# The modulation vectors of a two-block transformer: products on three engines in place of 32-column matmuls

## The chip, the cores and the metric

The kernel is one program on one core of one Trainium2 chip. The metric is the device time of one execution in microseconds (us), from the first to the last instruction and what the runtime lays around them. A core has TensorE (PE; its weight loads, which overlap the matmuls, are listed as PEld), VectorE (DVE), ScalarE (ACT), GpSimd (POOL) and SyncE (SP, which here issues most loads). Each engine runs its own instructions in order and waits for the others through semaphores. SBUF is the on-chip memory, PSUM the eight banks that TensorE writes.

## What is computed

Two blocks run one after the other on 512 latent tokens and 256 context tokens of width 1024, in float32. Each block is steered by modulation vectors: a conditioning vector goes through silu and is multiplied by a 1024 x 6144 matrix, and the product is cut into six vectors of 1024.

```python
s_lat = jax.nn.silu(c)
s_ctx = jax.nn.silu(c_ctx)
m_lat = jnp.split((s_lat @ w_mod[l] + b_mod[l])[:, None, :], 6, axis=-1)
m_ctx = jnp.split(s_ctx @ w_mod[l] + b_mod[l], 6, axis=-1)
h_lat = modulate(rmsnorm(x_lat, norm1_g[l]), m_lat[0], m_lat[1])
...
x_lat = x_lat + m_lat[2] * (mix_lat @ w_out[l])
h_lat = modulate(rmsnorm(x_lat, norm2_g[l]), m_lat[3], m_lat[4])
x_lat = x_lat + m_lat[5] * expert_choice_ffn(h_lat, ...)
```

The first block mixes tokens in four ways (neighbourhood attention, a gated delta net, differential attention, a Fourier transform) and goes through 16 experts. The second block has a state-space branch, an attention branch and a gated feed-forward net, and is modulated in the same way by `w_mod_2`.

## The kernel before

The kernel is a generator program. Pieces of work are Python generators; `weave` and `beside` interleave them in program order, and a list scheduler then orders each engine's instructions: of those whose inputs are there by its own model of time, the one that stands first in the program goes next. Matmul helpers record every operation under one line (L367), copies out of PSUM under L393 (ScalarE) and L395 (VectorE), loads under L398, so operations are told apart by their tiles.

The first two modulation vectors of the first block are made at the very start (`a_in`, bank tag `md`). All the others are made in `g_mods`: vectors 2, 3, 4, 5 of the first block and 0, 1, 3, 4, 2, 5 of the second. It runs beside `g_ft` (Fourier) and `g_na` (neighbourhood attention), and all three are woven with `g_dn`, the gated delta net. Behind them come `g_df` (differential attention) and `g_wo`, still beside `g_dn`; then the output projection, the choice of tokens, the experts with the context's part of the second block beside them, and the second block.

A vector is two blocks of 512 columns. `mod_rows` makes one: four loads of [128, 2, 512] (512 KB each) from a ring of three buffers in the pool `mods`, and eight float32 matmuls, each with a padded stationary of 32 columns (column 0 the latent's silu, column 1 the context's, the rest zero) and a 512-column slice of the weights as the moving operand. Contraction tile kt goes to the 32 PSUM partitions 32 (kt % 4), so one bank collects four partial rows for each of the two conditioning vectors. A copy (L393 and L395 in turn) takes the bank to SBUF. From there:

- `mod_bcast` (vectors used as a gate along the free axis): a matmul with the 0/1 matrix `k_sel` adds the four partial rows and spreads the sum over all partitions; VectorE adds the bias (L516).
- `mod_cols` (channels on partitions): four transposes a block (L490), a reduction (L491), the bias (L492).
- `mod_cols_pk` (channel 8 p + kt at [p, kt]): eight matmuls a block with a strided stationary of 64 columns into the bank `bigbank`, which `g_na` also takes its scores from; then a reduction (L503).
- the gates of the second block: `k_sel` again, the bias added in one partition (L644), stored to DRAM (`gtd`).

`g_dn` goes through 12 chunks, two at a time: `ind` inverts a triangular matrix of each chunk in a row of short steps (64x64 matmuls into `bank_dn`, a copy on ScalarE at L970, transposes at L957, products on GpSimd at L948 and additions on VectorE at L978), and `rec` takes the state from chunk to chunk (`bank_dnr`, one copy a chunk at L1001).

Of the kernel before, what the change touches and what calls it, by code (L numbers as in the profile page):

```python
# [9 lines left out]
F = np.float32  # L10

# ---------------------------------------------------------------- host layout
# [11 lines left out]
def _pack_cols(inp):  # L24
    parts, off = ([], []), [0, 0]
# [5 lines left out]
    g = lambda n: np.asarray(inp[n])  # L31
# [24 lines left out]
def _na_bias(rpb):  # L56
    rpb = np.asarray(rpb)[0]                          # [4, 15, 31]
# [14 lines left out]
    return np.ascontiguousarray(np.stack(out, 1).astype(F))      # [128, 12, 256]  # L72


def _consts():
# [3 lines left out]
    ang = np.concatenate([(t // 64)[:, None] * inv, (t % 64)[:, None] * inv], 1)    # [512, 16]  # L79
    cs = np.stack([np.cos(ang), np.sin(ang)], 1)                                    # [512, 2, 16]  # L80
# [23 lines left out]
    ang = np.stack([(t // 64)[:, None] * inv, (t % 64)[:, None] * inv], 1)          # [512, 2, 16]  # L104
    cs = np.stack([np.cos(ang), np.sin(ang)], 1)                                    # [512, 2, 2, 16]
    K["k_rope2"] = np.ascontiguousarray(cs.reshape(4, 128, 64).transpose(1, 0, 2)).astype(F)
    K["k_m"] = np.ascontiguousarray(np.concatenate(cols, 1)).astype(F)
    sel = np.zeros((128, 128))
    sel[[0, 32, 64, 96]] = 1.0
    K["k_sel"] = sel.astype(F)  # L110
# [21 lines left out]
class Arena:  # L132
    """SBUF of one core as a free list over one tile: alloc and free in program order."""
# [34 lines left out]
class Duo:  # L168
    """Two arenas as one."""
# [10 lines left out]
class Pool:  # L180
    """SBUF whose pieces are tiles of their own, all released together."""
# [12 lines left out]
class Buf:  # L194
    """A piece of an arena or a tile of a pool, seen as [128, *shape]."""
# [31 lines left out]
class Part(Buf):  # L227
    """A piece of a buffer."""
# [9 lines left out]
class Ring:  # L238
    """n equal buffers taken in turn."""
# [15 lines left out]
class Bag:  # L255
    """Equal buffers, given out and taken back; the one that came back first goes out first."""
# [12 lines left out]
    # buffers for a while, until shed  # L269
# [14 lines left out]
class Split:  # L284
    """A block of weights as two exact parts: part i of tile kt along the contraction."""
# [13 lines left out]
def weave(*gens):  # L299
    """Runs generators side by side; each yields the work it has put out, as a part of all of its own."""  # L300
# [9 lines left out]
def ranked(tc, gen, off):  # L310
    """gen's pieces, issued as if they stood off instructions further on."""
# [16 lines left out]
def beside(main, total, fill):  # L328
    """main's pieces, which yield total, and fill's, which yield 1, at the same pace."""
# [13 lines left out]
def filled(tc, main, fill):  # L343
    """main's pieces; each yields how much of fill goes in behind it, and maybe the instruction it stays behind."""
# [14 lines left out]
class KA:  # L359
# [5 lines left out]
    # ---------------------------------------------------------------- helpers  # L365
# [48 lines left out]
    # ---------------------------------------------------------------- set up  # L414
    def setup(self, cx):
# [14 lines left out]
        self.m2c_b = Buf(M, [4, 8, 2])                  # sh1, sc1, sh2, sc2 of the second block  # L430
        self.ab2_b = Buf(M, [3, 8])                     # norm gains: block 1 lat, ctx; block 2
# [12 lines left out]
    # a stage's SBUF as a free list  # L444
# [10 lines left out]
    # r ** -0.5 * f of a few columns  # L455
# [5 lines left out]
    # silu(c) columns of two vectors as a padded stationary [128, 8, 32]  # L461
# [2284 lines left out]
```

## Time and profile before

| what | value |
|---|---|
| timed runs, median of 3 | 3065.87 us (3064.37 to 3069.57) |
| profiled execution, first to last instruction | 3070.7 us |
| mean granted TensorE clock, share of full speed | 0.983 |
| TensorE matmuls busy | 2908.0 us, 95% |
| VectorE, ScalarE, GpSimd busy | 1341.8, 911.1, 631.7 us |
| stage with `g_mods` (223 to 455 us) | 232 us |
| stage with `g_df` (455 to 655 us) | 200 us |

The profiled execution lies 4.8 us (0.16%) above the median of the timed runs and 1.1 us above the highest of them. In the rows below, a group of instructions is given by line, engine and operation, then output <- inputs by tile names, shapes (partitions x elements), count, busy time in us, mean ns of one, and the idle time of the engine ahead of them with what ended it. A float32 matmul stands as two instructions. Busy time is a union: overlapping instructions count once. Shares are of the window that is named.

### The profile page before, as it was taken

Reading aid. Unit: us, or ns where it says so; the run is one execution under the profiler, and the core shown is the slowest. Engines: PE = TensorE matmul, PEld = TensorE weight load, DVE = VectorE, ACT = ScalarE, POOL = GpSimd, SP = SyncE. Lnnn points to the kernel's source line nnn. Section 1 sums busy time; section 2 is a strip of 40 time slices with the busy share of each in tenths; the row PEclk is TensorE's granted clock in tenths of the full one; section 3 lists DMA queues with packets and bytes.
Section 4 is the critical chain, followed back from the end, with each engine's and each line's share of the span. In section 5 each row is a group of like instructions: output and inputs, shape, how many; then the busy total and the mean of one; then the engine's idle time right before and its main releaser. Section 6 shows DMA issues by size and latency. Waiting matters only on the chain.

```text
span 3070.7 us, 42582 instructions
## 1 busy us (share of the span) xinstructions
PE 2908.0 (95%) x17172; PEld 1918.0 (62%) x17172; DVE 1341.8 (44%) x2673; ACT 911.1 (30%) x1855; POOL 631.7 (21%) x662
## 2 busy tenths in 40 slices
PE   7999999998999999899999989999999999999998
PEld 4894557756454544244343358787878778878887
DVE  5522546654221211011011057869696945364445
ACT  5511226532111010000000034445454444253333
POOL 3121225521000000000000023323232323242232
PEclk8999999999999999999999989999999999999999
DMA  7216660147979797999999943323332275242231
GB/s 261 75 46 200 206 197 23 35 155 290 371 311 386 318 368 321 423 431 430 431 430 431 430 152 102 103 84 100 86 105 82 87 251 174 94 153 96 96 102 57
DMA packets 255428, 652.01 MB, mean 212 GB/s; under 512 B 15672, under 2 KB 168760, under 8 KB 230656
## 3 DMA queue, kind: packets, MB, share of 16 engines
q1 hardware_dynamic: 212368, 600.95, 51.6%
q10 hardware_dynamic: 42864, 48.35, 4.7%
q8 instruction: 135, 2.21, 0.3%
q14 instruction: 61, 0.50, 0.1%
HBM read 627.61 MB, written 21.64 MB: 211 GB/s over the span
## 4 chain that ended last, share of the span: by engine, by line
PE 61%; DVE 8%; DMA 5%; ACT 2%; issue 1%; POOL 1%; POOLq 0%; DVEq 0%; ACTq 0%
PE bank_mm L367 25%; PE bigbank L367 22%; PE bank_pj L367 6%; PE bank_c L367 3%; DMA b<-in_w_down 2%; DMA l<-in_w_up 1%; PE bank_sm L367 1%; PE bank_y L367 1%; DMA wo<-in_w_down 1%; PE bank_mm L2146 1%; DVE mix L2395 1%; DVE base L2391 1%; DVE mix L2394 1%; DVE c L1929 1%; DMA l<-in_w_down 1%
## 5 line engine op out<-in xcount | busy, mean ns | idle before, releaser
L367 PE MATMUL bank_pj<-c,c 128*128 128x512 f32 (+2 forms) x1368 | 317.7, 375 | 0.0
L367 PE MATMUL bank_mm<-c,c 128*128 128x512 f32 (+1 forms) x1608 | 304.4, 347 | 2.5 <-DVE c L1929 1.3
L367 PEld LDWEIGHTS bank_mm<-c,c 128*128 128x128 f32 x1608 | 259.3, 191 | 42.1 <-DVE c L1929 1.7
L367 PEld LDWEIGHTS bank_pj<-c,c 128*128 128x128 f32 (+1 forms) x1368 | 225.1, 188 | 48.3 <-issue 15.4
L367 PE MATMUL bank_mm<-l 128*128 128x128 f32 (+3 forms) x944 | 229.1, 499 | 4.2 <-DVE l L395 2.0
L1928 ACT CAST c<-base 128x1024 fp32r<-128x1024 f32 x147 | 152.8, 1045 | 254.7 <-PE bigbank L367 105.7
L1929 POOL TENSOR_TENSOR c<-base,c 128x1024 fp32r<-128x1024 f32 x47 | 115.7, 2462 | 453.3 <-ACT c L1928 393.5
L367 PEld LDWEIGHTS bank_mm<-l 128*128 128x128 f32 (+2 forms) x944 | 155.6, 246 | 75.3 <-issue 66.6
L367 PE MATMUL bigbank<-l 128*64 128x512 f32 (+1 forms) x864 | 198.1, 586 | 4.5 <-DMA l<-in_w_up 2.8
L1929 DVE TENSOR_TENSOR c<-base,c 128x1024 fp32r<-128x1024 f32 x100 | 134.9, 1351 | 137.6 <-ACT c L1928 132.8
L367 PEld LDWEIGHTS bigbank<-l 128*64 128x64 f32 (+1 forms) x864 | 62.8, 141 | 117.9 <-issue 105.2
L1676 DVE TENSOR_TENSOR b<-l,bigbank 128x512 f32<-128x512 f32 x32 | 20.6, 684 | 255.7 <-PE bigbank L367 225.7
L367 PE MATMUL bank_c<-b 128*128 128x256 f32 (+3 forms) x496 | 119.2, 385 | 12.6 <-ACT b L1843 8.3
L1604 POOL TENSOR_TENSOR l<-l,ab 128x512 f32<-128x512 f32 x8 | 8.4, 1047 | 560.2 <-DVE l L1591 506.7
L367 PEld LDWEIGHTS bank_c<-b 128*128 128x128 f32 (+1 forms) x496 | 80.6, 194 | 54.8 <-issue 30.1
L367 PE MATMUL bigbank<-out,c 128*128 128x512 f32 x480 | 112.5, 394 | 2.4 <-ACT out L2489 1.8
L367 PE MATMUL bank_mm<-h,sp 128*128 128x512 f32 (+3 forms) x544 | 108.3, 388 | 4.2 <-ACT h L606 3.8
L367 PEld LDWEIGHTS bank_dn<-dn 64*64 64x64 f32 x1920 | 74.0, 134 | 56.4 <-issue 39.1
L367 PE MATMUL bigbank<-b,l 128*64 128x512 f32 x480 | 105.7, 593 | 2.3 <-DMA b<-in_w_up 1.2
L367 PEld LDWEIGHTS bigbank<-out,c 128*128 128x128 f32 x480 | 90.9, 190 | 22.9 <-ACT out L2489 2.0
L1600 ACT ACTIVATE l<-bank_mm,ab,ab 128x128 f32<-128x128 f32 x32 | 14.7, 458 | 292.6 <-DVE l L1602 292.4
L367 PEld LDWEIGHTS bank_mm<-h,sp 128*128 128x128 f32 (+1 forms) x544 | 85.9, 186 | 24.7 <-ACT h L606 4.0
(556 smaller groups left out, 5175.0 us busy)
## 6 DMA issues: line engine op xcount, KB each, us to landing
l<-in_w_up SPq DMA_DIRECT2D x25, 2048.0 KB, 10.6
l<-in_w_gate SPq DMA_DIRECT2D x25, 2048.0 KB, 9.6
l<-in_w_down SPq DMA_DIRECT2D x25, 2048.0 KB, 16.2
base<-in_w_in SPq DMA_DIRECT2D x90, 512.0 KB, 3.8
mods<-in_w_mod SPq DMA_DIRECT2D x80, 512.0 KB, 4.6
base<-in_w_up SPq DMA_DIRECT2D x18, 2048.0 KB, 8.6
wo<-in_w_gate SPq DMA_DIRECT2D x18, 2048.0 KB, 10.1
b<-in_w_gate SPq DMA_DIRECT2D x15, 2048.0 KB, 19.5
```

Of the source, the lines that this page charges most:

```text
L367: self.mm_ins = self.nc.tensor.matmul(out, l, r, start=start, stop=stop).ins
L1600: nc.scalar.activation(XG[:, kt], b[:, kk], AF.Identity, bias=b2[:, kt:kt + 1], scale=a2[:, kt:kt + 1])
L1604: nc.gpsimd.tensor_mul(sc, S, aff[:, :, ee, None].to_broadcast([128, 4, 2, 64]))
L1676: nc.vector.tensor_mul(hid[:, 512 * j:512 * j + 512], s, ac[1][:, j])
L1928: nc.scalar.copy(hi, raw)
L1929: (nc.vector if self.wn % 4 in self.losplit else nc.gpsimd).tensor_sub(lo, raw, hi.bitcast(F32))
L2146: nc.tensor.transpose(tb[:, z], p[:, 128 * (g0 + z):128 * (g0 + z) + 128], self.ident)
L2391: nc.vector.scalar_tensor_tensor(E[:, h], rw[:, h, 0], gc(1, 0, h), E[:, h], op0=OP.subtract, op1=OP.min)
L2394: nc.vector.tensor_scalar(W[:, h], cb[:, c, 0], gc(0, 0, h), None, op0=OP.mult)
L2395: nc.vector.scalar_tensor_tensor(W[:, h], cb[:, c, 1], gc(0, 1, h), W[:, h], op0=OP.mult, op1=OP.add)
```

## The change

`mod_rows` stays for the first two vectors. For all others a new function `mod_sums` takes its place. It multiplies each contraction tile [128, 512] of the weights by the conditioning column of that tile, one value a partition, and adds the eight products elementwise, so that one tile [128, 512] of sums over the contraction tiles is left, whose partitions have still to be added. Even tiles go to VectorE (one product, then three multiply-adds into `d`), odd tiles to ScalarE (four scaled copies), whose results GpSimd adds into `o`; a last GpSimd addition joins the two. The sum over partitions is a matmul with ones. A block is made for one conditioning vector at a time, so blocks that are wanted for the latent and the context (vectors 0 and 1 of the second block) load their weights twice.

```diff
+    def mod_sums(self, s, wdram, j, r):
+        nc, (wr, da, pa, pp) = self.nc, self.mr
+        wv = wdram.rearrange("(kt p) n -> p kt n", p=128)[:, :, j * 512:(j + 1) * 512]
+        d, o = da(), pa()
+        for k in range(0, 8, wr.per):
+            w = wr()
+            self.ld(w, wv[:, k:k + wr.per])
+            for i in range(wr.per):
+                kt = k + i
+                c = s[:, kt, r:r + 1]
+                if kt == 0:
+                    nc.vector.tensor_scalar(d, w[:, i], c, None, op0=OP.mult)
+                elif kt % 2 == 0:
+                    nc.vector.scalar_tensor_tensor(d, w[:, i], c, d, op0=OP.mult, op1=OP.add)
+                else:
+                    z = o if kt == 1 else pp()
+                    nc.scalar.activation(z, w[:, i], AF.Copy, scale=c)
+                    if kt > 1:
+                        nc.gpsimd.tensor_add(o, o, z)
+        nc.gpsimd.tensor_add(o, o, d)
+        return o
+    def mod_cols2(self, s, wdram, bname, j, rs, out):
+        nc, n = self.nc, len(rs)
+        t = self.bank((128, 8, n), self.md)
+        for h in range(2):
+            for r in rs:
+                o = self.mod_sums(s, wdram, 2 * j + h, r)
+                for c in range(4):
+                    self.mm(t[:, 4 * h + c, r:r + 1], o[:, c * 128:(c + 1) * 128], self.km("one", 1))
+        nc.vector.tensor_add(out[:, :, 0:n], t, ...)
     def mod_cols_pk(...)
-        t = self.big().rearrange("p (k g r) -> p k g r", k=8, g=4)
+        t = self.bank((128, 8), self.md)
         for h in range(2):
-            r = rows()
-            self.mod_rows(s, wdram, 2 * j + h, ring, r)
+            o = self.mod_sums(s, wdram, 2 * j + h, 0)
             for kt in range(8):
-                self.mm(t[64 * h:64 * h + 64, kt].rearrange("p g r -> p (g r)"), r[:, kt::8], self.ident)
+                self.mm(t[64 * h:64 * h + 64, kt:kt + 1], o[:, kt::8], self.km("one", 1))
     def mod_bcast(...)
-            r = rows()
-            self.mod_rows(s, wdram, 2 * j + h, ring, r)
+            r = self.mod_sums(s, wdram, 2 * j + h, 0)
             t = self.bank((128, 512), self.md)
-            self.mm(t, ksel, r)
+            self.mm(t, self.km("one"), r)
             o = out[:, h * 512:(h + 1) * 512]
             nc.vector.tensor_add(o, t, o)
+            yield 0.05
     def g_mods(self, tag, n):
-            wr, rows = Ring(P, [2, 512], n), Ring(P, [512], 2)
+            sums = [Ring(self.M, [512], k) for k in (1, 2)]
+            pp = Ring(P, [512], 2)
+            self.mr = [Ring(P, [2, 512], n)] + sums + [pp]
...
-                self.mod_cols(s2, wm, "b_mod_2", j, wr, rows, mc[:, i])
+                self.mod_cols2(s2, wm, "b_mod_2", j, (0, 1) if j < 2 else (0,), mc[:, i])
...
-                    self.mod_rows(s2, wm, 2 * j + h, wr, r)
+                    r, g = self.mod_sums(s2, wm, 2 * j + h, 0), pp()[0:1]
-                    self.mm(t, self.sel, r)
+                    self.mm(t, self.km("one"), r)
```

The rings are one buffer for `d`, two for `o`, two for ScalarE's products and, as before, three for the weights. `k_sel` and its load at the start are gone. `mod_bcast` yields after each block of 512 columns instead of after the vector. The rest of the diff takes comments out.

## Rows read from the trace of the kernel before

**Rows 1.** The page: span and number of instructions.

```profile
span 3070.7 us, 42582 instructions
```

**Rows 2.** Stages in one row each: length; busy us (instructions) by engine; clock, DMA share, GB/s.

```profile
223.00:455.00 232.00, 222.46 (x2160) 120.53 (x2156) 94.14 (x224) 56.75 (x175) 51.40 (x88) 0.99 0.63 206
455.00:655.00 200.00, 189.32 (x2396) 144.48 (x2393) 126.03 (x312) 110.42 (x305) 92.24 (x150) 0.98 0.12 42
...
655.00:1228.00 573.00, 539.07 (x2439) 275.90 (x2441) 133.21 (x280) 82.11 (x177) 54.22 (x54) 0.98 0.85 332
1228.00:1766.00 538.00, 499.57 (x2194) 210.41 (x2190) 62.99 (x107) 24.41 (x47) 3.14 (x3) 0.99 1.01 429
```

**Rows 3.** Groups of TensorE in the stage 223 to 455 us, by form.

```profile
L367 PE MATMUL bank_mm<-mods,ab 128*32 128x512 f32 x320 | 72.4, 610 | 4.7 <-DMA mods<-in_w_mod 4.7
L367 PE MATMUL bank_dn<-dn 64*64 64x64 f32 x880 | 45.4, 226 | 2.2 <-DVE base L1156 0.6 <-DVE dn L978 0.6 <-ACT dn L970 0.5
...
L367 PE MATMUL bank_mm<-mods,ab 128*128 128x512 f32 x16 | 9.9, 703 | 1.1 <-ACT mods L393 0.7 <-DVE mods L395 0.3
L367 PE MATMUL bigbank<-base,mods 128*64 128x128 f32 x64 | 8.8, 290 | 0.0
...
L367 PE MATMUL bank_mm<-l 128*128 128x512 f32 x16 | 7.2, 604 | 0.0
...
L490 PE MATMUL bank_mm<-base,mods 128*128 128x128 f32 x32 | 5.1, 283 | 0.0
```

**Rows 4.** The same view of the stage 455 to 650 us.

```profile
L367 PE MATMUL bank_mm<-l,dn 128*128 128x64 f32 x180 | 23.8, 276 | 0.0
```

**Rows 5.** Waits in 223 to 455 us: waiter <- releaser, total us, times, longest.

```profile
POOL dn L948 <- PE bank_dn L367: 80.2, 17, 10.4
...
ACT dn L970 <- PE bank_dn L367: 46.8, 21, 7.6
...
SPq L398 <- PE bank_mm L367: 125.5, 58, 6.7
```

**Rows 6.** The tile `mods`: ns min/median/max, first and last start us; then landing times.

```profile
L398 SPq DMA_DIRECT2D mods<-in_w_mod x80: 367/368/1624, 223.8 to 445.6; - x80
...
L395 DVE COPY mods<-bank_mm x10: 690/692/693, 263.8 to 451.7; 128x512 f32<-128x512 f32 x10
...
L644 DVE TENSOR_TENSOR mods<-mods,bank_mm x4: 675/676/676, 425.4 to 454.0; 1x512 f32<-1x512 f32 x4
...
DMA to landing us min/median/max: 3.7/4.6/9.0
```

**Rows 7.** Line 1001, one a chunk of `g_dn`: in 300:480, then in 460:680 us.

```profile
L1001 DVE COPY dn<-bank_dnr x5: 416/424/426, 314.5 to 469.2; 128x256 f32<-128x256 f32 x5
...
L1001 DVE COPY dn<-bank_dnr x8: 407/416/424, 469.2 to 677.6; 128x256 f32<-128x256 f32 x8
```

**Rows 8.** Groups of the whole run by form: operations like the added ones.

```profile
L1160 DVE TENSOR_SCALAR l<-l,base 128x512 f32<-128x512 f32 x16 | 8.6, 578 | 0.2
...
L2364 DVE SCALAR_TENSOR_TENSOR mix<-base,mix 128x512 f32<-128x512 f32 x32 | 22.1, 692 | 0.0
...
L1765 DVE SCALAR_TENSOR_TENSOR mix<-mix,mix 128x512 f32<-128x512 f32 x24 | 19.0, 792 | 7.0 <-ACT mix L1764 6.2
...
L2415 ACT ACTIVATE mix<-mix 128x512 f32<-128x512 f32 x8 | 5.0, 624 | 1.8 <-DVE mix L2413 1.7
...
L948 POOL TENSOR_TENSOR dn<-dn,a 128x256 f32<-128x256 f32 x60 | 45.4, 768 | 115.2 <-PE bank_dn L367 102.4 <-DVE dn L922 12.8
...
L1848 POOL TENSOR_TENSOR b<-b 128x512 f32<-128x512 f32 x16 | 16.5, 1042 | 176.1 <-ACT b L1843 119.9 <-PE bank_c L367 56.2
...
L1351 POOL TENSOR_TENSOR l<-l 128x512 f32<-128x512 f32 x8 | 11.6, 1445 | 32.0 <-DVE l L1350 32.0
```

**Rows 9.** Stretches near the start, same columns as rows 2.

```profile
10.00:20.00 10.00, 4.83 (x18) 1.24 (x16) 0.47 (x3) 2.60 (x5) 0.55 (x1) 0.69 1.03 415
...
40.00:50.00 10.00, 7.56 (x21) 5.41 (x21) 9.07 (x13) 8.51 (x14) 5.83 (x4) 0.66 0.80 277
```

More of the change, by code (lines that the diff above doesn't have):

```diff
@@ L107, in _consts @@
     K["k_m"] = np.ascontiguousarray(np.concatenate(cols, 1)).astype(F)
-    sel = np.zeros((128, 128))
-    sel[[0, 32, 64, 96]] = 1.0
-    K["k_sel"] = sel.astype(F)
     return K
@@ L492, in mod_cols @@
         nc.vector.tensor_add(out, out, self.col(bname, 8 * j, 8)[:, :, None].to_broadcast([128, 8, 2]))
-    def mod_cols_pk(self, s, wdram, bi, j, ring, rows, out):
+    def mod_sums(self, s, wdram, j, r):
[19 more added lines that the diff above has]
+        return o
@@ new lines, in mod_cols2 @@
+    def mod_cols2(self, s, wdram, bname, j, rs, out):
[6 more added lines that the diff above has]
+                    self.mm(t[:, 4 * h + c, r:r + 1], o[:, c * 128:(c + 1) * 128], self.km("one", 1))
+        nc.vector.tensor_add(out[:, :, 0:n], t, self.col(bname, 8 * j, 8)[:, :, None].to_broadcast([128, 8, n]))
@@ L496, in mod_cols_pk @@
+    def mod_cols_pk(self, s, wdram, bi, j, out):
         nc = self.nc
-        t = self.big().rearrange("p (k g r) -> p k g r", k=8, g=4)
+        t = self.bank((128, 8), self.md)
         for h in range(2):
-            r = rows()
-            self.mod_rows(s, wdram, 2 * j + h, ring, r)
+            o = self.mod_sums(s, wdram, 2 * j + h, 0)
             for kt in range(8):
-                self.mm(t[64 * h:64 * h + 64, kt].rearrange("p g r -> p (g r)"), r[:, kt::8], self.ident)
-        nc.vector.tensor_reduce(out, t[:, :, :, 0:2].rearrange("p c g r -> p c r g"), AX.X, OP.add)
@@ L504, in mod_cols_pk, with mod_bcast @@
-        nc.vector.tensor_add(out, out, self.col("b_mod_pk", 8 * bi, 8)[:, :, None].to_broadcast([128, 8, 2]))
-    def mod_bcast(self, s, wdram, bdram, j, ring, rows, out, ksel):
+                self.mm(t[64 * h:64 * h + 64, kt:kt + 1], o[:, kt::8], self.km("one", 1))
+        nc.vector.tensor_add(out[:, :, 0], t, self.col("b_mod_pk", 8 * bi, 8))
+    def mod_bcast(self, s, wdram, bdram, j, out):
         nc = self.nc
@@ L572, in a_in @@
         self.gt1_b, self.gt2_b = Buf(AB, [1024]), Buf(AB, [1024])
-        self.sel = Buf(AB, [128]).ap()
         self.md = "md"
@@ L582, in a_in @@
         self.ld(cx, I["ctx"][0].rearrange("(t p) d -> p t d", p=128), nc.scalar)
-        self.ld(self.sel, I["k_sel"], nc.scalar)
         s1, wm = self.s1b.ap(), I["w_mod"][0]
@@ L617, in g_mods @@
         with self.pool("mods") as P:
-            wr, rows = Ring(P, [2, 512], n), Ring(P, [512], 2)
+            sums = [Ring(self.M, [512], k) for k in (1, 2)]
+            pp = Ring(P, [512], 2)
+            self.mr = [Ring(P, [2, 512], n)] + sums + [pp]
             s1, wm = self.s1b.ap(), I["w_mod"][0]
             mp, a2 = self.mpk_b.ap(), self.a2_b.ap()
-            self.mod_bcast(s1, wm, I["b_mod"], 2, wr, rows, self.gt1_b.ap(), self.sel)
+            yield from self.mod_bcast(s1, wm, I["b_mod"], 2, self.gt1_b.ap())
+            self.mod_cols_pk(s1, wm, 0, 3, mp[:, 0])
             yield 0.1
-            self.mod_cols_pk(s1, wm, 0, 3, wr, rows, mp[:, 0])
-            yield 0.1
-            self.mod_cols_pk(s1, wm, 1, 4, wr, rows, mp[:, 1])
+            self.mod_cols_pk(s1, wm, 1, 4, mp[:, 1])
             nc.vector.scalar_tensor_tensor(a2, mp[:, 1, :, 0], 1.0, self.col("norm2_g_pk", 0, 8), op0=OP.add, op1=OP.mult)
             yield 0.1
-            self.mod_bcast(s1, wm, I["b_mod"], 5, wr, rows, self.gt2_b.ap(), self.sel)
-            yield 0.1
+            yield from self.mod_bcast(s1, wm, I["b_mod"], 5, self.gt2_b.ap())
             mc, a = self.m2c_b.ap(), self.ab2_b.ap()
@@ L638, in g_mods @@
                 for h in range(2):
-                    r, g = rows(), rows()[0:1]
-                    self.mod_rows(s2, wm, 2 * j + h, wr, r)
+                    r, g = self.mod_sums(s2, wm, 2 * j + h, 0), pp()[0:1]
                     t = self.bank((128, 512), self.md)
-                    self.mm(t, self.sel, r)
+                    self.mm(t, self.km("one"), r)
                     self.ld(g, I["b_mod_2"][0:1, 512 * (2 * j + h):512 * (2 * j + h) + 512], nc.scalar)
@@ L646, in g_mods @@
                 yield 0.1
+            for z in sums:
+                z.free()
     def chan(self, w, c, lat=True):
```

## Prediction

> **What bounds the kernel now.** I read the stages in single rows first, then the groups of TensorE in the stage concerned, then the waits there, the tile `mods`, and the pace of the delta net. The modulation vectors lie in 223 to 455 us, and there TensorE is busy 222.5 of 232 us (96%) while VectorE has 41%, ScalarE 24% and GpSimd 22% [rows 2]. The reader is to see one full engine beside three half-empty ones. The largest group on it is the change's own: 320 instructions of the 32-column matmuls, 72.4 us, more than the 45.4 us of the delta net's main group [rows 3]. The waits say the same from the other side: GpSimd's step L948 and ScalarE's copy L970 of the delta net wait 80.2 and 46.8 us for TensorE, and SyncE's loads 125.5 us for TensorE to release weight buffers [rows 5]. The delta net sets the end: its copy once a chunk comes every (469.2 - 314.5) / 4 = 38.7 us in this stage and every (677.6 - 469.2) / 7 = 29.8 us behind it, and its last one, at 677.6, lies behind the end of the stage of differential attention at 655 [rows 2, 7]. Behind that TensorE is 94% busy until 1228, and from there to 1766 the DMA engines are full at 429 GB/s [rows 2]; those loads follow buffers that the experts release, so I let a gain at 678 us pass to the end whole.
>
> **TensorE, removed and added.** The 20 blocks cost 72.4 us, the transposes 5.1 and the strided matmuls into `bigbank` 8.8 [rows 3]: 86.3 us. The eight spreading matmuls (9.9 us for 16 instructions) stay, with ones in place of `k_sel`. New are six vector-and-row pairs of eight one-column products, 48 matmuls or 96 instructions, with a stationary of 128 columns. The nearest row has that stationary and 64 moving columns, 23.8 / 180 = 0.132 us an instruction [rows 4]: 12.7 us. The strided products stay 64 instructions with one column in place of 128: at most the old 8.8 us. From below, the 64x64 group's 45.4 / 880 = 0.052 us [rows 3] gives 8.3 us for all 160. I take the upper end, as weight loads set it: 86.3 - 21.5 = 65 us less (78 at most), so 158 us stay of 222.5.
>
> A rule speaks against this gain. A 32-column instruction took 72.4 / 320 = 0.226 us against 7.2 / 16 = 0.45 us for a 128-column one of equal length [rows 3], so two ran at a time. The Trainium skill, page "TensorEngine Tiling (Array Packing)", section "Theoretical Speedup", gives up to four at a time for a dimension of 32 or less. By that the 320 would be worth 36 us, and removing them would free about 29 us in all; the row decides.
>
> **The other engines.** `mod_sums` runs 24 times: four blocks each for the two spread vectors, the two strided ones and the two gates, and twelve for the second block's columns (two vectors for latent and context, two for latent only). VectorE gets 24 x (0.578 + 3 x 0.692) = 64 us (71 us with 0.792) and loses ten copies, 6.9 us [rows 6, 8]: 94 becomes about 151. ScalarE gets 96 x 0.624 = 60 us [rows 8]: 57 becomes 117 at most. GpSimd gets 96 additions at 1.042, 100 us, or at 1.445, as beside a busy VectorE, 139 us [rows 8]: 51 becomes 151 to 190. I take 1.1 us, nearer the first, as the row of plain operands. So no engine is left above 190 us of the 232; TensorE, VectorE and GpSimd lie near 155 each.
>
> **The loads.** 80 become 96. They now go out every (445.6 - 223.8) / 79 = 2.81 us; with three buffers a buffer turns in 8.4 us, of which 4.6 are landing and 3.8 the wait for TensorE [rows 5, 6]. The new readers are one VectorE and one ScalarE operation, side by side, 0.69 us at the longer [rows 8]; with about one more such operation queued ahead I take 1.6 us. From below it is 0.7, from above the old 3.8. A turn is then 6.2 us and a load goes every 2.07 us (1.8 to 2.8), which is 253 GB/s; loads near the start ran at 415 [rows 9]. The 96th goes out at 223.8 + 95 x 2.07 = 420.5. The last gate's addition ran 8.4 us behind the last load [rows 6]; the same gives 429, 25 us earlier than 454.0. The loads of the experts stand behind these 96 in SyncE's queue, which empties earlier, too. The dropped load of `k_sel` and the four more yields I cost at nothing: the first is 222 us ahead of the stage, the second only spread the same work.
>
> **The sum.** The gain is the delta net's. Before, its pace gives (455 - 223) / 38.7 = 6.0 chunks in the first stage and 7.5 behind it. After, the first stage ends at 429 and the pace in it lies between 38.7 (TensorE's relief is lost again in the queues of the other engines) and 29.8 (the pace beside differential attention, where the other three are 63, 55 and 46% busy and TensorE 95% [rows 2]). At 38.7 the last copy comes at 672, 6 us earlier; at 29.8 at 624, 53 us earlier. I take three fifths of the way, 33.4 us: TensorE is then at 158 / 206 = 77%, well below that later stage, but VectorE and GpSimd are at about 73%, above it. That makes 6.2 chunks by 429 and 7.3 x 29.8 = 217 us more: 646, or 31 us earlier. Differential attention, which starts when `mods` and its buffers are freed, took 200 us with this pace beside it and would end near 630, so the delta net stays last. By the profiled execution 3070.7 - 31 = 3040 [rows 1]; that execution lies 4.8 us above the median of the timed runs, so the median becomes 3065.9 - 31 = 3035 us.
>
> **Rivals.** *The chain gets no faster.* TensorE's busy time holds the tails of its pipeline, so part of the 96% may be the chain's own latency, and the waits on TensorE turn into waits behind 0.7 to 1.1 us operations elsewhere. For it: VectorE's and GpSimd's shares above. Against it: L948's 80.2 us of waiting for TensorE [rows 5]. Pace 38.7 gives 3060; with the loads at their old pace too, 3066.
>
> *Slower, by the hand-over between blocks.* There is one buffer `d`: the first VectorE product of a block waits for the closing GpSimd addition of the block before it, which waits for ScalarE's last product and the addition ahead of it; and ScalarE's first product waits for the ones-products of two blocks earlier, in TensorE's queue. Behind each waiting product stand the delta net's own copies and additions, since these engines go in order. Over two additions of 1.1 us with one or two 0.77 us steps of L948 between them [rows 8], a block could take 12 to 13 us in place of 4 x 2.07 = 8.3. At 13 us the vectors end at 223.8 + 312 + 8 = 544. By then differential attention has not begun, but the delta net has done (544 - 223) / 33.4 - 6.0 = 3.6 chunks more than before. Its main group alone costs 45.4 / 6.0 = 7.6 us a chunk [rows 3], so of the later stage's 189 us of TensorE [rows 2] 27 are gone at least, and 54 if its other groups cost as much again, which I take (an estimate). The other 135, at that stage's 95%, take some 140 us: it ends at 684, not 655, which is 29 us later: 3095. It decides from where 24 blocks + 8 + 140 pass 655 - 224 = 431: at 11.8 us a block. Against it: the scheduler interleaves by readiness, and three weight buffers cover one late block.
>
> *The clock.* Near the start, where TensorE was busy 48 and 76%, the granted clock was 0.69 and 0.66, part of the time at 1.2 instead of 2.4 GHz [rows 9]; in the stage it was 0.99 [rows 2]. At 0.66 the 158 us become 158 x 0.99 / 0.66 = 237, more than the 222.5 of now, and the stage gains nothing: 3070. The Trainium skill, page "TensorE: Matmul & The Clock Gate", section "Why this matters for your kernels", asks for no idle gaps between bursts of matmuls, else the clock falls back. By that rule this is the way it would go, if the idle comes in long pieces; at 77% with short ones I don't expect it.
>
> **Chances.** Forecast 0.60 (gain 6 to 53, so 3013 to 3060); chain no faster 0.15, half of it under 6 us; hand-over 0.17; clock 0.08, half of it beyond +6 us. Faster by over 0.2% (6 us, about what a measurement of this kernel can tell from no change): 0.60 + 0.08 = 0.68. Slower: 0.17 + 0.04 = 0.21. Within: 0.11. The range runs from 3008 (53 us, and 5 for the cheaper one-column products) to 3080, half-way into the hand-over's case, and leaves about 0.15 out.
>
> **What would show it.** Right: TensorE near 77% in the shortened stage, its waits small; loads of `mods` every 2.1 us, the last near 420; L1001 every 33 us there; the wait of L948 for TensorE well under 80 us. Wrong: loads every 2.8 us or more, VectorE or ScalarE waiting for GpSimd at the head of a block, GpSimd's additions above 1.4 us, a clock under 0.9, or L1001 at 38 us with TensorE idle.

## The result and the profile after

The changed kernel takes 3143.48 us (3141.82 to 3146.61) against 3067.07 us (3064.37 to 3069.57) for the kernel before: a ratio of 1.025, 95% interval 1.0235 to 1.0264. It is slower by 76.4 us. The forecast was 3035, its range ended at 3080: the prediction was wrong in sign and in size. The profiled execution shown below spans 3144.5 us, 73.8 more than that of before [rows 1].

The stages of the kernel after, one row each; columns as in [rows 2], with the engines in the order PE, PEld, DVE, ACT, POOL. The end of the first stage has moved, so the second is cut where differential attention now begins.

```profile
223.00:455.00 232.00, 174.52 (x1676) 129.25 (x1672) 142.25 (x239) 87.37 (x207) 145.87 (x152) 0.75 0.58 183
455.00:542.00 87.00, 58.31 (x584) 43.53 (x583) 45.62 (x87) 31.38 (x73) 51.86 (x54) 0.70 0.51 161
542.00:742.00 200.00, 185.14 (x2062) 135.27 (x2062) 120.62 (x289) 104.45 (x287) 84.19 (x131) 0.97 0.16 54
742.00:1300.00 558.00, 527.01 (x2404) 271.59 (x2405) 129.58 (x276) 80.66 (x173) 47.77 (x50) 0.98 0.85 333
1300.00:1840.00 540.00, 499.53 (x2206) 211.13 (x2206) 64.02 (x110) 25.81 (x50) 4.19 (x4) 0.99 1.01 429
```

The stage with `g_mods` has grown from 232 to about 319 us. No engine is full in it: TensorE is busy 75% of the first row and 67% of the second, VectorE 61 and 52%, GpSimd 63 and 60%. The granted clock is 0.75 and 0.70, where it was 0.99. Behind 542 the rows look like those of before again.

The delta net's copy once a chunk (L1029, L1001 of before): seven of them in 300 to 607, then all twelve.

```profile
L1029 DVE COPY dn<-bank_dnr x7: 407/424/425, 324.8 to 605.9; 128x256 f32<-128x256 f32 x7
...
L1029 DVE COPY dn<-bank_dnr x12: 407/420/425, 324.8 to 753.6; 128x256 f32<-128x256 f32 x12
```

The first seven chunks stand (605.9 - 324.8) / 6 = 46.9 us apart, the last five gaps (753.6 - 605.9) / 5 = 29.5. The slow pace is new (38.7 before [rows 7]), the fast one is that of before. The last copy has moved by 753.6 - 677.6 = 76.0 us; the span has grown by 73.8. So the loss arises ahead of this copy, and hardly any of it is made good behind it.

The tile `mods` in the kernel after (minimum, median, maximum in ns; first and last start), and the landing of its loads:

```profile
L395 SPq DMA_DIRECT2D mods<-in_w_mod x96: 367/368/1697, 223.6 to 521.4; - x96
L508 ACT ACTIVATE mods<-mods,ab x72: 708/722/744, 231.3 to 527.4; 128x512 f32<-128x512 f32 x72
L505 DVE SCALAR_TENSOR_TENSOR l<-mods,ab,l x72: 732/752/1828, 231.4 to 526.9; 128x512 f32<-128x512 f32 x72
L510 POOL TENSOR_TENSOR dn<-dn,mods x72: 1255/1268/1814, 232.1 to 530.0; 128x512 f32<-128x512 f32 x72
...
L670 DVE TENSOR_TENSOR mods<-mods,bank_mm x4: 664/672/677, 498.4 to 534.8; 1x512 f32<-1x512 f32 x4
...
DMA to landing us min/median/max: 3.6/4.2/7.1
```

A load goes out every (521.4 - 223.6) / 95 = 3.13 us, 12.5 us a block; the vectors are done at 535, not at 454.

Waits in 223 to 540 us, kernel after; columns as in [rows 5].

```profile
PE bank_mm L364 <- POOL dn L511: 57.6, 20, 6.2
...
POOL dn L510 <- ACT mods L508: 36.3, 18, 5.4
...
DVE l L503 <- POOL dn L511: 33.7, 15, 5.9
```

Each row gives the waiter, what ended its wait, the total in us, how often, and the longest. The first row has no counterpart before: TensorE waits 57.6 us for L511, GpSimd's closing addition of a block, and the matmuls into `bank_mm` that wait are the ones-products. The reader is to see one of these waits in the timelines of two engines (start, length, instruction, idle time ahead of it); first TensorE, then GpSimd:

```profile
322.18 0.96 PE L364 MATMUL bank_dnr<-dn 64*64 64x64 f32 x16
323.26 0.71 PE L364 MATMUL bank_dn<-dn,a 128*128 128x128 f32 x4
328.35 2.08 PE L364 MATMUL bank_mm<-dn,base 128*128 128x512 f32 x2 [4.38 <-POOL dn L511]
```

```profile
324.90 1.25 POOL L510 TENSOR_TENSOR dn<-dn,mods 128x512 f32<-128x512 f32 x1
326.12 0.84 POOL L948 TENSOR_TENSOR dn<-dn 128x256 f32<-128x256 f32 x1
326.92 1.38 POOL L511 TENSOR_TENSOR dn<-dn,l 128x512 f32<-128x512 f32 x1
```

From 323.97 TensorE stands 4.38 us before a ones-product at the head of its queue, until the closing addition ends at 328.30. Ahead of that addition GpSimd has a last product to add and a delta-net step. TensorE goes in order, so whatever of the delta net stands behind the ones-product stands still with it. How much of it would have been ready, this piece doesn't show; the runs below bear on it.

### The profile page after: what moved, and what is told of

Same layout as the page of the kernel before. It is cut to its first block, busy times and chain, and to the rows that moved or that the text cites. A ratio compares the mean times of both kernels' runs of the same rounds, so it can differ in the third digit from the quotient of the medians.

```text
span 3144.5 us, 42485 instructions
## 1 busy us (share of the span) xinstructions
PE 2903.4 (92%) x16916; PEld 1958.4 (62%) x16916; DVE 1424.9 (45%) x2749; ACT 966.6 (31%) x1941; POOL 763.8 (24%) x758
## 4 chain that ended last, share of the span: by engine, by line
PE 60%; DVE 7%; DMA 5%; ACT 1%; issue 1%; POOL 1%; POOLq 0%; DVEq 0%; ACTq 0%
PE bank_mm L364 24%; PE bigbank L364 22%; PE bank_pj L364 6%; PE bank_c L364 3%; DMA b<-in_w_down 2%; PE bank_sm L364 1%; PE bank_y L364 1%; DMA wo<-in_w_down 1%; PE bank_mm L2174 1%; DVE mix L2423 1%; DVE base L2419 1%; DVE mix L2422 1%; DVE c L1957 1%; DMA l<-in_w_down 1%; DMA l<-in_w_up 0%
## 5 line engine op out<-in xcount | busy, mean ns | idle before, releaser
L364 PE MATMUL bank_mm<-l 128*128 128x128 f32 (+4 forms) x992 | 237.9, 490 | 5.5 <-DVE l L392 2.0
L364 PEld LDWEIGHTS bank_mm<-l 128*128 128x128 f32 (+2 forms) x992 | 163.3, 243 | 77.0 <-issue 65.7
L364 PE MATMUL bank_dn<-dn 64*64 64x64 f32 x1920 | 109.4, 251 | 16.0 <-DVE dn L1006 6.0
L364 PEld LDWEIGHTS bank_dn<-dn 64*64 64x64 f32 x1920 | 87.7, 157 | 46.7 <-issue 18.4
L510 POOL TENSOR_TENSOR dn<-dn,mods 128x512 f32<-128x512 f32 x72 | 97.4, 1353 | 50.3 <-ACT mods L508 36.3
```

Source lines behind the costliest of these rows:

```text
L364: self.mm_ins = self.nc.tensor.matmul(out, l, r, start=start, stop=stop).ins
L510: nc.gpsimd.tensor_add(o, o, z)
```

## The experiments

Two theories at the start. *In-order wait*: the loss is TensorE's standing before ones-products whose sum GpSimd closes late. *Load of the other engines*: the delta net's own copies and additions queue behind products of 0.7 to 1.3 us on VectorE, ScalarE and GpSimd, whatever TensorE waits for. The clock is a third. Of the kernels that only take a part out or move it there is one run each; runs of one kernel lay up to 10 us apart (3041.6 to 3051.6 for one of the last three), so differences of a few us between single runs say nothing. The median of the kernel before, run beside the experiments, was 3067.8 to 3069.3 us.

**The relief alone.** The kernel before with most of its 32-column matmuls cut to eight columns.

```diff
-            self.mm(b[32 * g:32 * g + 32, :], s[:, kt, :], wv[:, kt % ring.per, :], kt < 4, kt >= 4)
+            if self.md != "mm":
...
+            elif kt == 0:
+                self.mm(b, s[:, 0:4, :].rearrange("p a b -> p (a b)"), wv[:, 0, :])
+            else:
+                self.mm(b[32 * g:32 * g + 32, :8], s[:, kt, :], wv[:, kt % ring.per, :8])
```

> The kernel before, with TensorE relieved and no engine loaded: of the eight 32-column matmuls of a block one stays, with 128 columns, and seven shrink to 8 moving columns, so the modulation vectors are not computed; loads, copies and transposes stay. TensorE loses about 2 us of each of 20 blocks, some 40 us. If the loss of the changed kernel comes from waits for its closing additions or from the queues of the other engines, this one has neither and becomes 15 to 40 us faster (3027 to 3052). If a TensorE that is less densely used drops its clock and loses what it gained, the granted clock of the stage falls below 0.9 here too and the time stays at 3067 or above.

It took 3054.08 us, 15 less than before, the least that was expected. The groups of TensorE in 223 to 455 us:

```profile
L367 PE MATMUL bank_mm<-mods,ab 128*128 128x512 f32 x56 | 34.6, 720 | 0.5 <-ACT mods L393 0.4
...
L367 PE MATMUL bank_mm<-mods,ab 128*32 128x8 f32 x280 | 15.5, 187 | 4.9 <-DMA mods<-in_w_mod 4.9
```

These two hold what was 72.4 + 9.9 us [rows 3]: 50.1, so 32 us of TensorE were taken away and gave 15 us. Relief of TensorE is worth something, and nothing about it explains a loss. About half of it was lost again: up to the delta net's last copy TensorE idled 31.0 us in place of 22.3, and its clock was 0.96 in place of 0.99 (table below).

**The ones-products without their wait.** The kernel after, its ones-products reading a constant in place of the sums.

```diff
-                    self.mm(t[:, 4 * h + c, r:r + 1], o[:, c * 128:(c + 1) * 128], self.km("one", 1))
+                    self.mm(t[:, 4 * h + c, r:r + 1], self.ident, self.km("one", 1))
... (and so in mod_cols_pk, mod_bcast and the gates)
```

> The changed kernel with every ones-product reading the identity in place of the finished sums (the modulation vectors are left out; products, additions and loads all stay). TensorE no longer waits for GpSimd's closing addition. If that wait, with the delta net queued behind it in order, is the loss, its 57.6 us go, the clock of the stage comes back above 0.95 and the time falls to 3040 to 3080. If the queues of VectorE, ScalarE and GpSimd are the loss, it stays above 3110. If the thin use of TensorE alone drops the clock, the clock stays below 0.85 with the wait gone, and the time at 3100 or more.

It took 3085.92 us: 57.6 less than after, as many us as the wait had, though not the same ones, as the table below shows. The time is 6 us above what the theory of the wait was given, and the clock of the stage stayed at 0.79, where that theory asked for 0.95 and the theory of the clock for less than 0.85 (but 3100 us or more). All products, additions and 96 loads are still there. The stage, and what VectorE still waits for:

```profile
223.00:455.00 232.00, 188.90 (x1977) 138.17 (x1977) 167.56 (x288) 104.72 (x250) 172.27 (x173) 0.79 0.66 209
```

```profile
DVE l L503 <- POOL dn L511: 30.5, 18, 3.8
```

So the hand-over through the one buffer `d` is still there (33.7 after), in a kernel that is only 17 us above the one before; three quarters of the loss went with the wait on TensorE. The edit takes away one thing more, ScalarE's wait for the ones-products to release the sums, which was 5.4 us in after.

**The load alone.** The same, with the old 32-column matmuls put back on the weights, their result unread.

```diff
+                    b = self.bank((128, 512), self.md)
+                self.mm(b[32 * (kt % 4):32 * (kt % 4) + 32, :], s[:, kt, :], w[:, i], kt < 4, kt >= 4)
...
```

> As the run with ones-products from the identity, and the old 32-column matmuls put back beside the products on the same loaded weights, into a bank that nobody reads (about 3.6 us of TensorE for each of 24 blocks, 87 us). It loads the other three engines and keeps TensorE dense. Theory of the clock: granted clock back at 0.97 or more, and the time below that of the run without the matmuls if the clock was the loss. Theory of the queues: still slower than before by 40 us or more (3107 or above) with a full clock. Theory of the waits: 3070 to 3100, slower than without the matmuls by part of their 87 us.

3133.15 us. The clock in 223 to 455 us is 0.93 again, TensorE is busy 214 us, and the kernel is 64 us slower than before: 47 us more than with the same products, additions and loads and TensorE relieved. By its number that is what the theory of the queues was given (3107 or above), but the run doesn't decide for it: it has 24 blocks of the old matmuls where the kernel before has 20, and up to the delta net's last copy TensorE is busy 476.2 us against 432.3 before. So 44 of the 64 us are TensorE's own work. What is left for the load of the other engines is the 17 us of the run without the matmuls.

**The closing addition moved to TensorE.** Two accumulating ones-products in place of one addition and one product, and a second `d`.

```diff
-        nc.gpsimd.tensor_add(o, o, d)
-        return o
+        return o, d
...
-            self.mm(t, self.km("one"), r)
+            for i, z in enumerate(r):
+                self.mm(t, self.km("one"), z, i == 0, i == 1)
```

> The changed kernel without the closing addition on GpSimd: the ones-products go over VectorE's and ScalarE's partial sums one after the other and add in PSUM; two buffers of each. GpSimd has 72 additions in place of 96, and VectorE's first product of a block no longer waits for GpSimd; TensorE has twice the ones-products (some 25 us more). Theory of the waits: one link of 1.3 us less in the chain, TensorE's wait for GpSimd falls from 57.6 to 20 to 40 us and the time to 3095 to 3125. Theory of the queues: 24 x 1.3 = 31 us less on GpSimd give 3115 to 3135. Theory of the clock: no change beyond 10 us.

3146.93 us, no better, and the time that only the theory of the clock had foreseen (no change). Part of the wait went, and part changed its name:

```profile
POOL dn L510 <- ACT mods L508: 64.5, 22, 10.7
...
PE bank_mm L364 <- POOL dn L510: 43.8, 19, 5.0
```

TensorE now waits for GpSimd's last product addition, the additions for ScalarE, and there are twice as many ones-products. Up to the delta net's last copy TensorE idles 80.2 us in place of 101.0 and is busy 452.0 in place of 429.6: what the shorter wait gave, the doubled ones-products took. Taking out the closing addition and the single `d` doesn't take the wait away; the sum still comes late.

**No additions on GpSimd.** The odd tiles' products are still made on ScalarE, but nothing adds them (they are left out of the sums); ones over VectorE's sums alone, two `d`.

```diff
-                    if kt > 1:
-                        nc.gpsimd.tensor_add(o, o, z)
-        nc.gpsimd.tensor_add(o, o, d)
-        return o
+        return d
```

> The changed kernel with all of GpSimd's additions left out, and with them the odd contraction tiles from the sums: the ones-products read VectorE's partial sums (two buffers), ScalarE's products are made and not used. GpSimd loses 96 additions of 1.27 to 1.35 us, some 125 us, and the hand-over to it is gone. Theory of the late closing sums: what is waited for is GpSimd, so TensorE's wait falls from 57.6 to under 20 us, loads go every 2.6 us or faster, time 3045 to 3080. If the products on VectorE and ScalarE and their queues are the loss as well, the wait turns into one for VectorE and the time stays at 3090 or more.

3069.91 us, equal to the kernel before (3068.65), as the theory of the late sums had it. With the 96 GpSimd additions thus goes nearly the whole loss, 3143.5 - 3069.9 = 73.6 us; the second `d` is not what did it, for the runs before and behind this one have it, too, and take 3146.9 and 3135.4. Even so the kernel only breaks even: 3069.9 - 3054.1 = 15.8 us worse than the relief alone, with the products on VectorE and ScalarE, 13.3 us of waits for VectorE's sums, 16 loads more and a stage clock of 0.84.

```profile
223.00:455.00 232.00, 194.12 (x2160) 146.45 (x2159) 150.99 (x319) 117.27 (x274) 69.03 (x102) 0.84 0.74 241
```

**80 loads in place of 96.** Both conditioning vectors are made from one load; two buffers for `d`.

```diff
+                for q, d, o in zip(rs, ds, os):
+                    c = s[:, kt, q:q + 1]
...
```

> The changed kernel with one load for both conditioning vectors where both are wanted: 80 loads in place of 96, the same 24 blocks of products, two buffers of each sum. If the stage is set by the loads (3.13 us each), the last vector is done 16 x 3.1 = 50 us earlier, near 488, and the time is 3095 to 3110. If it is set by the blocks of products and additions (13 us each), nothing moves beyond 10 us: 3133 to 3153.

3135.39 us, 8 less than after. The loads stretch to 504 all the same, (504.1 - 222.0) / 79 = 3.57 us each:

```profile
L395 SPq DMA_DIRECT2D mods<-in_w_mod x80: 367/368/588, 222.0 to 504.1; - x80
```

The 24 sums set the pace, not the loads.

**All products on VectorE.** No ScalarE copies, no GpSimd additions, two buffers for `d`; everything is computed.

```diff
-                elif kt % 2 == 0:
+                else:
                     nc.vector.scalar_tensor_tensor(d, w[:, i], c, d, op0=OP.mult, op1=OP.add)
-                else:
-                    z = o if kt == 1 else pp()
-                    nc.scalar.activation(z, w[:, i], AF.Copy, scale=c)
-                    if kt > 1:
-                        nc.gpsimd.tensor_add(o, o, z)
-        nc.gpsimd.tensor_add(o, o, d)
-        return o
+        return d
```

> The changed kernel with all eight products of a block on VectorE (one product, seven multiply-adds), none on ScalarE or GpSimd; the output is complete. VectorE gets 24 x (0.49 + 7 x 0.75) = 138 us, some 72 us more than in the changed kernel. Theory of the hand-over: no engine waits for another before the ones-products, so TensorE's wait falls under 25 us although VectorE is fuller, and the time is 3080 to 3115. Theory of the queues: VectorE, which the delta net needs at every step, is nearly full, and the time is at or above 3143.

3108.83 us, 35 less than after, with VectorE at 178 of 232 us; the theory of the hand-over had asked for 3080 to 3115. TensorE's waits for the sums, in 223 to 540 us:

```profile
PE bank_mm L364 <- DVE dn L505: 10.6, 6, 5.0
...
PE bank_mm L364 <- DVE l L505: 6.1, 2, 4.6
```

With a single engine doing all eight products there is no hand-over among three queues, and the loads end at 486.7, not 521.4.

**The ones-products issued a piece later.** The changed kernel with a yield between the sums and the ones-products, which are also put behind the matmul that was issued last.

```diff
                 o = self.mod_sums(s, wdram, 2 * j + h, r)
+                yield 0.05 / n
+                with self.tc.issue_after(self.mm_ins):
...
```

> The changed kernel with its complete output; the ones-products of a tile are issued one piece of the block later, so that GpSimd's closing addition has more time before TensorE's queue reaches them. If the loss is the wait of TensorE's in-order queue for a late sum, and the sums are late by less than a piece, the wait falls from 57.6 us to under 25 us, and the time comes to 3085 to 3115 (the bound is the 3085.9 of the run in which the ones-products wait for nothing). If GpSimd itself is too slow for the pace (four additions of 1.3 us a tile), the wait only stands one piece later, and the time stays at 3135 or more.

3124.85 us, between the two ranges expected, with a wait above the 25 us of the first: 18.6 us less than after, with the wait 17.8 less:

```profile
PE bank_mm L364 <- POOL dn L511: 39.8, 16, 4.4
```

Side by side: TensorE's wait for the sums in 223 to 540 us, then its idle time, busy time and clock from 223 us to the delta net's last copy, which stands in the seventh column. Behind that copy all these kernels have the same 11166 matmul instructions to run.

| kernel | wait, us | idle, us | busy, us | clock | time, us | last copy, us |
|---|---|---|---|---|---|---|
| before | none | 22.3 | 432.3 | 0.99 | 3067.1 | 677.6 |
| relief alone | none | 31.0 | 408.5 | 0.96 | 3054.1 | 662.4 |
| after | 57.6 | 101.0 | 429.6 | 0.83 | 3143.5 | 753.6 |
| 80 loads | 46.4 | 94.8 | 425.2 | 0.82 | 3135.4 | 743.0 |
| ones a piece later | 39.8 | 82.0 | 427.7 | 0.84 | 3124.9 | 732.7 |
| all on VectorE | 16.7 | 73.6 | 417.4 | 0.84 | 3108.8 | 714.0 |
| ones read a constant | 0 | 68.2 | 403.6 | 0.88 | 3085.9 | 694.8 |
| no GpSimd additions | 13.3 | 52.7 | 399.1 | 0.89 | 3069.9 | 674.8 |
| doubled ones-products | 43.8 | 80.2 | 452.0 | 0.84 | 3146.9 | 755.2 |
| old matmuls put back | none | 38.4 | 476.2 | 0.95 | 3133.2 | 737.6 |

From after down to the run with a constant, about one us of time goes with one us of wait, down to a rest of 17 us, although these kernels differ in much else. The last three fall out of the row: two have more work for TensorE, and the one without GpSimd's additions lies some 29 us below it.

The rows of before, of after and of the run with a constant:

```profile
223.00:677.60 454.60, 432.32 (x4689) 275.38 (x4685) 229.28 (x555) 171.16 (x489) 151.44 (x244) 0.99 0.42 138
...
223.00:753.60 530.60, 429.57 (x4429) 314.51 (x4425) 314.99 (x631) 226.82 (x575) 284.36 (x340) 0.83 0.42 134
...
223.00:694.80 471.80, 403.55 (x4366) 294.00 (x4366) 315.49 (x629) 225.82 (x571) 288.91 (x334) 0.88 0.46 149
```

With the wait gone the stretch is 58.8 us shorter, but only 32.8 us of that is idle time. Other waits grew as this one went (for L1006, from 5.4 to 13.2 us in 223 to 540), and 26.0 us are matmuls that ran faster, at a clock of 0.88 in place of 0.83. That time and wait fell by the same 57.6 us is chance.

**Four column groups next to each other.** The relief had a cheaper form. [Rows 3] show 32-column matmuls at 72.4 / 320 = 0.226 us, two at a time, and a load brings two contraction tiles, so two column groups. Here the kernel before keeps its matmuls and loads four contraction tiles at a time: by 256 columns in three buffers, by 512 in two, by 256 in four (the row buffers kept elsewhere in the last two).

```diff
-            wr, rows = Ring(P, [2, 512], n), Ring(P, [512], 2)
+            wr, rows = Ring(P, [4, 512], 2), Ring(self.M, [512], 2)
...
...
+                for k in (0, 4):
+                    wv = ring()
+                    self.ld(wv, wd[:, k:k + 4, j * 512 + hh * w_:j * 512 + (hh + 1) * w_])
+                    for g in range(4):
+                        self.mm(b[32 * g:32 * g + 32, hh * w_:(hh + 1) * w_], s[:, k + g, :], wv[:, g, :], k == 0, k == 4)
```

> The kernel before with the same bytes a load cut otherwise: four contraction tiles by 256 columns in place of two by 512, so that the four column groups stand next to each other in TensorE's queue. If four groups run at a time in place of two, the 72 us of 32-column matmuls become about 36; relieving TensorE by some 40 us alone gave 15 us, so 3052 to 3060 is expected. If only two run at a time whatever the order, or if rows of 1 KB in place of 2 KB slow the loads, the time stays within 4 us of 3067 or rises above 3072.

> The kernel before with its 32-column matmuls, complete output; the modulation weights are loaded four contraction tiles at a time by 512 columns, into two buffers, so that four matmuls for four different column groups stand next to each other in TensorE's queue, each with 512 columns. If four adjacent column groups are what shortened them in the run with 256 columns (48.4 us for all, against 72.4 us), the same shows here, and with half the loads the time is 3035 to 3055. If the turn of only two buffers limits the loads (they then end after 445), the time is 3060 or more.

> As the run with loads of four contraction tiles by 256 columns (3046.33), complete output, with four weight buffers in place of two, the rows kept elsewhere. If the turn of the buffers still set the end of the loads there (427.1), they end earlier by 5 us or more, and the time is 3030 to 3042. If TensorE's own work sets it, the time is within 5 us of 3046.

256 columns: 3046.33 us, ratio 0.9926 (0.991 to 0.9943), more of a gain than was expected; its 32-column matmuls take 48.4 us, 24.0 less. The kernel had three buffers, not the two that the expectation of the last run gives it. 256 columns, four buffers: 3046.04, 0.9923 (0.9907 to 0.994); its loads end at 415.2 in place of 427.1 and the time is the same, so the turn of the buffers isn't what limits the time. 512 columns: 3038.79 us (3038.01 to 3040.73), ratio 0.9903 (0.9889 to 0.9918), better than both kernels of the case. A piece of TensorE's timeline, first before, then with 512 columns:

```profile
300.97 1.05 PE L367 MATMUL bank_mm<-mods,ab 128*32 128x512 f32 x4
```

```profile
303.44 1.92 PE L367 MATMUL bank_mm<-mods,ab 128*32 128x512 f32 x16
```

The same instruction, 0.26 us apiece in a run of four and 0.12 in a run of sixteen. An instruction of this length with 128 columns took 0.45 [rows 3], so four ran at a time. In the stage 223 to 455 us, with 512 columns:

```profile
L367 PE MATMUL bank_mm<-mods,ab 128*32 128x512 f32 x320 | 43.6, 624 | 3.0 <-DMA mods<-in_w_mod 3.0
```

72.4 - 43.6 = 28.8 us less on TensorE, and 3067.82 - 3038.79 = 29.0 us less time.

## Why the prediction was wrong

**TensorE as the bound: right.** Taking work off it pays, 28.8 us giving 29.0 in the last experiment and 32 giving 15 in the first. The sum's 31 us for 65 us of relief was of that order.

**The prices of the added TensorE work: right at the full clock.** In a piece of after that ran at a granted clock of 1.00, eight one-column instructions take 1.05 us, 0.131 each, where 0.132 was taken. Over 223 to 540 us, most of it at a lower clock, the group comes to 18.3 / 96 = 0.191.

```profile
399.47 1.05 PE L364 MATMUL bank_mm<-base,dn 128*128 128x1 f32 x8
```

```profile
L364 PE MATMUL bank_mm<-base,dn 128*128 128x1 f32 x96 | 18.3, 312 | 30.1 <-POOL dn L511 30.1
```

**The failed step: the pace of the delta net.** The sum let it lie between 38.7 us a chunk ("TensorE's relief is lost again in the queues of the other engines") and 29.8. 38.7 was no bound. It measured 46.9, because the change adds waits to the engine that was to be relieved, and with them its clock fell. The prediction named what waits on VectorE and ScalarE, and that ScalarE's first product waits for ones-products "in TensorE's queue". It never asked the reverse: what the ones-products wait for, and that the delta net's matmuls stand behind them in TensorE's order. Those waits, put at nothing in the sum, are 57.6 us, and without them the time is 3085.9. The second term that failed is the 158 us that TensorE was to be busy: they were priced at a clock of 0.99, and it ran at 0.75 and 0.70 (see the clock, below).

**The hand-over rival: half right.** It had a block at 12 to 13 us (12.5 measured), the vectors done at 544 (535) and 3095 us; the run without TensorE's wait took 3086. But it let the delta net go on at 33.4 us a chunk meanwhile and so missed the larger part. Against it I set three weight buffers and an order by readiness. Neither prevented it: the buffers wait for VectorE, which waits for `d`, and the order is fixed from modelled durations, while the additions ran longer than they cost anywhere in [rows 8] with plain operands.

**The loads.** 2.07 us each was the forecast, 3.13 the measurement. A turn of three buffers is 9.4 us; less 4.2 for landing, 5.2 are the wait for the readers, and 1.6 were taken. SyncE's queue names the readers, the products of VectorE:

```profile
SPq L395 <- DVE l L505: 113.9, 58, 6.5
SPq L395 <- DVE l L503: 83.1, 22, 8.0
```

**The operations.** In 223 to 540 us, by form:

```profile
L510 POOL TENSOR_TENSOR dn<-dn,mods 128x512 f32<-128x512 f32 x72 | 97.4, 1353 | 50.3 <-ACT mods L508 36.3 <-ACT dn L508 6.9 <-DVE l L505 3.5
```

```profile
L508 ACT ACTIVATE mods<-mods,ab 128x512 f32<-128x512 f32 x72 | 51.6, 721 | 43.0 <-DMA mods<-in_w_mod 21.9 <-POOL dn L510 14.1 <-PE bank_mm L364 5.4
```

```profile
L505 DVE SCALAR_TENSOR_TENSOR l<-mods,ab,l 128x512 f32<-128x512 f32 x72 | 65.6, 911 | 11.4 <-DMA mods<-in_w_mod 11.0
```

GpSimd 1.35 in place of 1.1, ScalarE 0.72 in place of 0.62, VectorE 0.91 in place of 0.69 (0.75 in the median). All three were mis-sized on the same side, by 16 to 32%. The totals were in bounds all the same: up to 139 us were allowed for GpSimd's additions, and they took 97.4 + 1.27 x 24 = 128. No engine came near full; a block of 12.5 us with its hand-overs set the pace of the vectors.

**The clock.** Given 0.08, with idle time in long pieces as its condition. No idle piece for the sums is longer than 6.2 us, and yet the clock fell, to between the two levels on the mean. Single stretches of after:

```profile
300.00:320.00 20.00, 17.32 (x134) 12.91 (x130) 10.79 (x22) 7.93 (x21) 5.84 (x5) 0.67 0.52 163
...
460.00:480.00 20.00, 13.29 (x68) 10.69 (x68) 11.27 (x19) 8.34 (x21) 10.91 (x10) 0.50 0.65 209
...
560.00:580.00 20.00, 18.29 (x171) 12.92 (x168) 12.16 (x24) 12.93 (x35) 7.18 (x12) 1.00 0.08 28
```

At 0.50 all of the 20 us ran at 1.2 GHz; from 560 all ran at 2.4. The Trainium skill, page "TensorE: Matmul & The Clock Gate", section "Why this matters for your kernels", asks for no idle gaps between bursts of matmuls. The trace agrees: with these waits the stage stands at 0.75 and 0.70, without them it stood at 0.99. I had set the rule aside. What it costs is seen in the same groups, two rows of after and one of before:

```profile
L364 PE MATMUL bank_dn<-dn 64*64 64x64 f32 x784 | 49.1, 273 | 13.0 <-DVE dn L392 5.9 <-DVE dn L1006 3.5 <-ACT dn L390 2.1
...
L364 PE MATMUL bigbank<-l 64*128 64x256 f32 x56 | 17.7, 564 | 0.0
```

```profile
L367 PE MATMUL bigbank<-l 64*128 64x256 f32 x64 | 15.2, 413 | 0.3 <-DVE ab L503 0.3
```

The first is 0.063 us an instruction against 45.4 / 880 = 0.052 [rows 3], a mean of 273 ns against 226; the second 0.316 against 15.2 / 64 = 0.238. For the whole program TensorE's busy time is 2903.4 us against 2908.0: nearly all of the 65 us taken off came back as slower matmuls. An estimate from the rows up to the last copy says the same: busy time multiplied by the clock is 432.3 x 0.99 = 428 us before and 429.6 x 0.83 = 357 after, 71 less, about what was forecast; at 0.99 those 357 would have taken 360, so the clock cost some 69. How much of the 76 us a full clock would have saved is open all the same, since faster matmuls would have stood before the sums the longer. The wait and the low clock come together, but not wholly: with the wait gone the stage still stands at 0.79 and 0.84. The one kernel with the clock back at 0.93 had it through 32-column matmuls that cost more than they could give back; a change of the clock alone wasn't tried.

**The balance.** Up to the delta net's last copy, and as TensorE spent it: work taken off -72 and the lower clock +69 (both estimates from above), idle time 101.0 - 22.3 = +79, together the 76. Of the idle time 57.6 us are the wait for L511, and most of the rest are shorter waits for VectorE and ScalarE. By runs: the relief of the first experiment -15; products on VectorE and ScalarE, more loads and a lower clock +16; GpSimd's additions with the wait for them +74. The run with a constant splits the last into 16 and 58, but the 58 hold the clock that came back with the wait.

**Behind the stage.** That a shift of the delta net's last copy passes whole to the end was right: 76.0 us there, 73.8 in the span.

**The rule on tiling.** The prediction set the Trainium skill's up to four tiles at a time (page "TensorEngine Tiling (Array Packing)", section "Theoretical Speedup") against the row's two, and let the row decide. For the price of what is removed that was right. As a reading of the chip it was not: by the rule 36 us were possible (an estimate), and 43.6 were measured once four groups stood side by side. The row showed the order of issue, not the array.

## What to carry to other kernels

When work leaves a full engine but a small remainder stays on it, ask what that remainder now waits for: in an engine that goes in order, a late operand stops all that is queued behind it, and here 58 us of such waiting went with 58 us of time, about half of it idle time and half slower matmuls, because TensorE's clock fell as well. Price a chain over three engines by its latency for one block, not by the busy shares. And before moving work off a full engine, see whether it runs there as it could: issuing the same matmuls four column groups at a time gave 29 us, without moving anything.

## What the hardware showed beyond that

VectorE's multiply-add of 128x512 took 911 ns in the mean beside GpSimd's additions, and up to 1828. In the kernel with all products on VectorE and none of these additions the same operation took 787, and in the one that differs from after by these additions and a second `d`, 800. That GpSimd's work is what stretches it is inferred from such pairs:

```profile
L505 DVE SCALAR_TENSOR_TENSOR dn<-mods,ab,dn 128x512 f32<-128x512 f32 x84 | 66.1, 787 | 7.1 <-DMA mods<-in_w_mod 6.3
```

```profile
L505 DVE SCALAR_TENSOR_TENSOR l<-mods,ab,l 128x512 f32<-128x512 f32 x36 | 28.8, 800 | 9.3 <-DMA mods<-in_w_mod 9.0
```

The Trainium skill, page "GPSIMD Engine Reference", section 4.1 "Engine selection", has a two-input operation about twice as slow on GpSimd as on VectorE. The medians here, 1268 ns for GpSimd's addition and 752 for VectorE's multiply-add, give 1.7, though the two aren't the same operation and each ran beside the other.
